# A third Winograd unit for the gates of a hybrid encoder layer, with the layer norm and the first rows reordered

## The chip, the core and the metric

The kernel runs on one core of a Trainium2 chip. The metric is the device time of one execution in microseconds (us). The engines that matter here are TensorE (PE; its weight loads, PEld, are listed apart and overlap the matmuls), VectorE (DVE), ScalarE (ACT), GpSimd (POOL) and SyncE (SP), which issues most of the DMAs.

## What is computed

One encoder layer on 512 tokens of width 1024: a gated pair of mixers (an S5 state-space branch and a gMLP branch), then cross-attention to 256 memory tokens, then a SwiGLU feed-forward network of width 2816. Only the first part is touched by the change:

```python
n = rms_norm(h, mix_norm_g[i])
proj = n @ w_in[i]                                  # 1024 x 4608
xa = proj[..., :OFF_U]                              # 512 columns, to S5
zu = proj[..., OFF_U:OFF_V]                         # 1024
zv = proj[..., OFF_V:OFF_GA]                        # 1024
gate_a = sigmoid(proj[..., OFF_GA:OFF_GB])          # 1024
gate_b = sigmoid(proj[..., OFF_GB:])                # 1024
ya = s5_branch(xa, ...)                             # ends y * sigmoid(gelu(y) @ w_glu)
yb = sgu_branch(zu, zv, ln_g, ln_b, w_s, bias)      # gelu(zu) * (w_s @ layer_norm(gelu(zv)) + bias)
merged = gate_a * (ya @ w_proj_a[i]) + gate_b * (yb @ w_proj_b[i])
h = h + merged @ w_out[i]
```

All matrices are float32.

## The kernel before

**Products.** Each float32 operand is split in two parts, hi and lo (`split`, L85 a ScalarE copy, L86 a VectorE subtraction), and each block product is three matmuls: hi by hi, hi by lo, lo by hi. `tokm` makes a result with tokens on the partitions (tiles `pt`, L393): the rows of 128 tokens are stationary, 512 columns of the weight stream by. `feat` makes a result with features on the partitions (tiles `pf`): one call gives 256 columns for all 512 tokens by 48 matmuls of 512 columns, and calls `evac` for each half. Where a product is large enough, the kernel uses Winograd's form of Strassen's scheme: a unit of 512 columns in seven block products instead of eight, each of 24 matmuls of 256 columns (`product`, L1221; tiles `gx`, `gv`, `gq` for the gates). The block products 1, 2, 4 and 7 read the features xn as they are; 3, 5 and 6 read sums of quarters of xn that `gate_sum` prepares. Their weights are blocks of w_in, or sums of these in the tile `gw`, made by VectorE or by an accumulating DMA.

**Stages, in TensorE's order.** First rows (rms norm, transposition `ptr` to features, L554); first half of zv, xa and second half of zv; the gate of a (`ga_evac`, four `feat` passes: sigmoid, tile `gas`, stored to the DRAM scratch `gad`); the spatial mixing (`psv`, L1185); zu, w_proj_b (result in `part`); the gate of b in two Winograd units, multiplied into `part` by `gate_put`; w_glu; w_proj_a, whose evacuation reads the gate of a back from `gad` (`gat`); then w_out, attention and the feed-forward network, which the change does not touch. The S5 branch runs as a side program: a generator whose steps are issued between the others', as `tick` counts the time of the matmuls issued. `later(n, f)` issues f after n of these time units. The S5 steps named below are `pw` (transposes, copied by ScalarE to `inx` or `ex`, L930), `pz` (copied to `zh`, L953), `pk` (copied to `ks`, L881), and the DMAs `kd` and `tt` (L889 to L897) on POOL's queue.

**Order.** Weights come in the order of `plan`: a block is loaded three blocks ahead (`LOADS`) or as many as its entry says, at most seven (`FAR`), and split two ahead (`SPLITS`). SP issues DMAs in the order in which they were issued in the program, POOL likewise. `plan_sums` spreads over the plan the sums that attention and the last projection need: a SP load or copy of a block into a DRAM tile `qsum`, then an accumulating load on POOL (L311). Its list of places says at which block of the plan each begins. `in_order` pins instructions to program order; all others a scheduler may move.

**The first rows.** `first_rows` broadcasts the norm's gain g by two matmuls (`pg`), copies each half to `g_mix` (L615) and then scales the half of row 0 (L616). In the loop over rows 1 to 3 each is scaled and turned. The log step of S5 comes by a DMA into a part of `slab` and is exponentiated at L726.

**The spatial mixing.** After the second half of zv, `row_weights` sums the rows of w_s. During the gate of a, `mixing_setup` (at `later(5)`) transposes w_s (`pws`), brings the layer norm's gain and bias to the partitions (`pgb`, `gbc`), scales `mix` (the broadcast row sums) by the bias of the norm (L1159) and adds `sgu_bias` by an accumulating DMA on POOL (L1160). `layer_norm(t)` at `later(1 + t)` subtracts the mean of row tile t (L1118), takes squares (`sq`, L515), a power on POOL (L1123), and scales (L1124). `psv` then takes the eight heads in turn; VectorE evacuates each with `mix` added (`sv`, L1186).

Of the kernel before, what the change touches and what calls it, by code (L numbers as in the profile page):

```python
# [52 lines left out]
def hybrid_layer_kernel(  # L53
# [29 lines left out]
    def split(dst_hi, dst_lo, src):  # L83
# [3 lines left out]
        if pinned[0]:  # L87
            in_order(hi)
            in_order(lo)


    pinned = [False]
# [130 lines left out]
    GATES = [(w_in, OFF_GB), (w_in, OFF_GB + 512)]  # L223
    ORDER = ((1, 0), (2, 0), (5, 0), (6, 0), (1, 1), (7, 0), (2, 1), (5, 1), (6, 1), (3, 0), (7, 1), (4, 0), (4, 1), (3, 1))
    gate_place = [None]

    def plan_gates():

        kh = KD // 2
        for q, i in ORDER:  # L230
            w, c0 = GATES[i]
# [12 lines left out]
            def make(q=q, i=i, b=b, got=got):  # L244
                t, b11 = (gate_place[0](2 * i + j) for j in range(2))
                if q in (2, 3):
                    return halves(got.pop("raw"))
                if q == 5 and i == 0:
                    nc.vector.tensor_tensor(t, t, got.pop("b12"), ALU.add)
# [3 lines left out]
                elif q == 6:  # L253
# [4 lines left out]
            loads = {1: [(5, whole(2 * i + 1, b(0, 0)))], 2: [(LOADS, plain(b(1, 0)))],  # L258
                     5: [(8, whole(2 * i, b(0, 0))),
                         (4, plain(b(0, 1), nm="b12")) if i == 0 else  # L260
                         (6, lambda i=i, b=b: nc.gpsimd.dma_start(gate_place[0](2 * i), b(0, 1), accum_op=ALU.add)),
# [72 lines left out]
    for c0 in range(0, D, 256):  # L334
        plan_feat(w_in, OFF_GA + c0, KD)
# [5 lines left out]
    for c0 in range(0, SW, 256):  # L341
        plan_feat(w_glu, c0, SW // P)
# [10 lines left out]
    for i in range(4):  # L353
# [7 lines left out]
    plan_sums([(5 + 3 * i, 3) for i in range(8)] + [(50 + 2 * i, 2) for i in range(7)] +  # L361
              [(85 + 3 * i, 3) for i in range(3)] + [(122 + 5 * i, 4) for i in range(14)])
# [69 lines left out]
    def tokm(w, c0, act, nk, evac, ntok=NT, last=2, kpt=2, hook=None, cut=None, t0=0):  # L432
# [19 lines left out]
        for t in toks:  # L452
# [5 lines left out]
            else:  # L458
                tok_block(ps[t], t, held, act, kpt, full, nw == last, True)
# [88 lines left out]
    def to_feat(src, hi, lo, tsl, full=None, skip=None, part=(0, 1), behind=None):  # L548

        for q in part:  # L550
            ps = aux("ptr", (P, 4, P))
            for j in range(4):
                k = 4 * q + j
                tr = nc.tensor.transpose(ps[:, j, :], src[:, k * P:(k + 1) * P], ident)  # L554
                if behind is not None:
                    in_order(tr)
            if q != skip:
                split(hi[:, 4 * q:4 * q + 4, tsl], lo[:, 4 * q:4 * q + 4, tsl], ps)
# [48 lines left out]
    def first_rows():  # L607
# [4 lines left out]
        idles(2)  # L612
        r = rms_factor(row_sums(xt[:, 0, :]))
        for i in range(2):
            in_order(nc.scalar.copy(g_mix[:, HALF[i]], pg[i]))  # L615
            in_order(nc.vector.scalar_tensor_tensor(xt[:, 0, HALF[i]], xt[:, 0, HALF[i]], r, pg[i], ALU.mult, ALU.mult))  # L616
# [1304 lines left out]
```

## Time and profile before

| | |
|---|---|
| runs | 875.28 us median of 3 (872.94 to 876.23) |
| profiled execution | 875.6 us; span of its instructions 873.8 us |
| mean granted TensorE clock | 0.991 |
| instructions | 14852 |
| TensorE busy | 860.3 us (98%), 5897 matmuls |
| VectorE, ScalarE, GpSimd busy | 648.0 (74%), 475.6 (54%), 108.8 (12%) |
| DMA | 155.40 MB, 178 GB/s on the mean |

The stages that the change touches, with the busy time of each engine in them (from the profile's windows):

```profile
0.00:22.60 22.60, 19.15 (x70) 14.30 (x71) 11.95 (x29) 13.09 (x29) 3.47 (x13) 0.85 0.81 237
22.60:97.80 75.20, 75.20 (x419) 61.37 (x418) 64.78 (x127) 38.41 (x68) 3.67 (x3) 0.98 0.61 161
97.80:154.00 56.20, 56.20 (x541) 46.50 (x540) 42.05 (x89) 37.64 (x64) 29.32 (x43) 1.00 0.68 184
161.20:265.40 104.20, 104.18 (x714) 85.23 (x712) 73.20 (x87) 54.35 (x64) 22.33 (x46) 1.00 0.53 138
265.40:305.80 40.40, 40.40 (x345) 40.40 (x345) 31.39 (x34) 26.18 (x37) 3.86 (x3) 1.00 0.72 194
```

A row gives the stretch in us from the span's start, its length, and the busy time and number of instructions of PE, PEld, DVE, ACT and POOL; then the granted TensorE clock (1.00 is full), the share of DMA time, and GB/s. The rows are the start; zv and xa; the gate of a; zu and w_proj_b; the gate of b. In the rows of timelines below, the start and the duration come first, then engine, line, operation and tiles, and in brackets the idle time of that engine ahead of it with what ended it. In rows of the chain it is start, duration and what the chain ran through. In grouped rows, busy time and mean duration in ns follow the count, then idle time ahead of the group.

### The profile page before, as it was taken

How to read it: one execution, taken by the hardware profiler on the slowest of the kernel's cores; microseconds unless marked ns; L12 is line 12 of the kernel's file. 1: busy time of each engine (PE TensorE's matmuls, PEld its weight loads, DVE VectorE, ACT ScalarE, POOL GpSimd, SP SyncE). 2: the span in 40 equal slices, each digit the busy share in tenths (PEclk: the TensorE clock that was granted, in tenths of full speed). 3: DMA queues.
4: the chain of work that ended last, by engine and by line, in shares of the span. 5: the costliest groups of instructions: out<-in, count | busy, mean ns of one | idle time of the engine just before them, and what ended most of it. 6: DMA issues, size and time to landing. Idle time of an engine off the chain costs nothing.

```text
span 873.8 us, 14852 instructions
## 1 busy us (share of the span) xinstructions
PE 860.3 (98%) x5897; PEld 764.8 (88%) x5897; DVE 648.0 (74%) x897; ACT 475.6 (54%) x704; POOL 108.8 (12%) x157
## 2 busy tenths in 40 slices
PE   8999999999999999999999999999999999999996
PEld 6788888878889988889899878999999999888875
DVE  5599679867748768679658656867877778889875
ACT  5453875267436544557547444645545454655663
POOL 1000066100611010110000001001111111000000
PEclk8999999999999999999999999999999999999998
DMA  7457559844647687934688144557799777467672
GB/s 235 121 154 223 115 179 234 203 121 153 173 121 197 162 223 202 287 113 167 204 253 218 54 151 110 145 135 177 173 222 228 201 194 167 135 205 229 197 249 85
DMA packets 110119, 155.40 MB, mean 178 GB/s; under 512 B 8969, under 2 KB 77089, under 8 KB 109986
## 3 DMA queue, kind: packets, MB, share of 16 engines
q1 hardware_dynamic: 91746, 128.27, 45.1%
q0 software_dynamic: 18016, 25.66, 18.5%
q8 instruction: 46, 0.75, 0.3%
q10 hardware_dynamic: 288, 0.52, 0.2%
q14 instruction: 23, 0.19, 0.1%
HBM read 148.70 MB, written 37.20 MB: 213 GB/s over the span
## 4 chain that ended last, share of the span: by engine, by line
PE 95%; DVE 1%; DMA 1%; SPq 1%; ACT 0%; issue 0%; POOLq 0%; POOL 0%; ACTq 0%
PE pf L393 27%; PE pt L393 18%; PE px L1221 12%; PE dx L393 7%; PE pq L1221 6%; PE dq L393 3%; PE pv L1221 3%; PE gx L1221 3%; PE qx L1221 2%; PE dv L393 2%; PE py L1015 1%; DMA slab<-in_s_log_step_dram 1%; PE gq L1221 1%; PE ptr L554 1%; PE po L393 1%; PE qq L1221 1%
## 5 line engine op out<-in xcount | busy, mean ns | idle before, releaser
L86 DVE TENSOR_TENSOR wlo<-wraw,whi 128x1024 fp32r<-128x1024 f32 (+1 forms) x135 | 160.0, 1185 | 82.4 <-ACT whi L85 82.0
L85 ACT CAST whi<-wraw 128x1024 fp32r<-128x1024 f32 (+1 forms) x135 | 138.0, 1023 | 145.0 <-PE pf L393 46.9
L393 PE MATMUL pf<-xn,whi 128*128 128x512 f32 x320 | 100.4, 393 | 0.0
L1221 PE MATMUL px<-fn,whi 128*128 128x256 f32 x480 | 83.3, 276 | 0.0
L1221 PEld LDWEIGHTS px<-fn,whi 128*128 128x128 f32 x480 | 72.5, 188 | 0.3 <-ACT u L1776 0.2
L393 PEld LDWEIGHTS pf<-xn,whi 128*128 128x128 f32 x320 | 59.5, 188 | 12.7 <-issue 0.7
L86 DVE TENSOR_TENSOR wlo<-b,whi 128x1024 fp32r<-128x1024 f32 x40 | 48.9, 1222 | 28.9 <-ACT whi L85 28.9
L85 ACT CAST whi<-b 128x1024 fp32r<-128x1024 f32 x40 | 42.2, 1054 | 51.2 <-PE px L1221 27.1
L1221 PE MATMUL px<-fn,wlo 128*128 128x256 f32 x240 | 66.4, 277 | 0.0
L393 PE MATMUL pf<-xn,wlo 128*128 128x512 f32 x160 | 62.6, 392 | 0.0
L393 PE MATMUL dx<-whi,s 128*128 128x512 f32 x170 | 53.9, 392 | 1.4 <-ACT whi L85 1.0
L1221 PE MATMUL pq<-s,whi 128*128 128x256 f32 x320 | 55.1, 276 | 0.0
L86 DVE TENSOR_TENSOR wlo<-t,whi 128x1024 fp32r<-128x1024 f32 x30 | 36.7, 1224 | 19.9 <-ACT whi L85 19.9
L85 ACT CAST whi<-t 128x1024 fp32r<-128x1024 f32 x30 | 31.6, 1053 | 35.8 <-PE pv L1221 12.6
L1221 PEld LDWEIGHTS pq<-s,whi 128*128 128x128 f32 x320 | 48.3, 188 | 0.1
L393 PE MATMUL pt<-whi,xn 128*128 128x512 f32 x128 | 45.4, 430 | 1.9 <-ACT xn L85 1.9
L1221 PEld LDWEIGHTS px<-fn,wlo 128*128 128x128 f32 x240 | 45.1, 188 | 0.0
L1221 PE MATMUL pq<-s,wlo 128*128 128x256 f32 x160 | 44.2, 277 | 0.0
L393 PEld LDWEIGHTS dx<-whi,s 128*128 128x128 f32 x170 | 31.7, 188 | 8.5 <-ACT whi L85 1.2
L393 PEld LDWEIGHTS pf<-xn,wlo 128*128 128x128 f32 x160 | 30.1, 188 | 6.3 <-issue 0.2
L311 POOL DMA_DIRECT2D dsum<-in_w_down_dram x12 | 13.3, 1108 | 163.3 <-DMA dsum<-in_w_down_dram 163.3
L393 PE MATMUL dx<-wlo,s 128*128 128x512 f32 x85 | 33.1, 390 | 0.0
(478 smaller groups left out, 2342.4 us busy)
## 6 DMA issues: line engine op xcount, KB each, us to landing
wraw<-in_w_in_dram SPq DMA_DIRECT2D x35, 512.0 KB, 5.4
dsum<-in_w_down_dram SPq DMA_DIRECT2D x20, 512.0 KB, 5.7
wraw<-dsum SPq DMA_DIRECT2D x20, 512.0 KB, 3.9
b<-in_w_gate_dram SPq DMA_DIRECT2D x15, 512.0 KB, 4.8
b<-in_w_up_dram SPq DMA_DIRECT2D x15, 512.0 KB, 4.5
wraw<-in_w_down_dram SPq DMA_DIRECT2D x15, 512.0 KB, 4.0
dsum<-in_w_down_dram POOLq DMA_DIRECT2D x10, 512.0 KB, 7.7
dsum<-dsum POOLq DMA_DIRECT2D x10, 512.0 KB, 5.5
```

What stands on the lines that cost most here:

```text
L85: hi = nc.scalar.copy(dst_hi, src)
L86: lo = nc.vector.tensor_tensor(dst_lo, src, dst_hi.bitcast(F32), ALU.subtract)
L311: plan[j + step][1].append((0, lambda d=dst, x=more: nc.gpsimd.dma_start(d, x, accum_op=ALU.add)))
L393: nc.tensor.matmul(ps, a[x], b[y], start=start and i == 0, stop=stop and i == 2, skip_group_check=free)
L554: tr = nc.tensor.transpose(ps[:, j, :], src[:, k * P:(k + 1) * P], ident)
L1015: in_order(nc.tensor.matmul(ps[64 * j:64 * j + 64, :], a, b, start=g % 4 == k == 0, stop=k == 2, tile_position=(0, 64 * j), skip_group_che ...
L1221: nc.tensor.matmul(ps[:, j, :], a[x], b[y], start=start and j == k == i == 0, stop=k == 3 and i == 2, skip_group_check=True)
```

## The change

It has four parts. (1) The second half of the columns of the gate of a leaves the `feat` passes and becomes a third Winograd unit beside the two of the gate of b: `GATES` has three entries, `ORDER` 21 products and the two passes of w_glu among them. The unit's tiles for weights and the bank of its fifth product are shared with those of the second unit of b, and its results go through SP to `gad`. (2) `layer_norm(t)` follows the evacuation of row tile t of zv's second half, `mixing_setup` is put off by 4.6 units from before that second half, and only two `feat` passes of the gate of a are left ahead of `psv`. (3) In `first_rows` row 0 is scaled ahead of the copies of g; the copies, the split of the first block and the features of row 0 are pinned in a new order; rows 1 to 3 are scaled behind the features of the row before; the split of the third weight block, the first matmuls of the last two weight blocks, the Exp of the log step and the row sums of w_s are held behind named instructions. (4) The places of `plan_sums` are moved.

```diff
-    GATES = [(w_in, OFF_GB), (w_in, OFF_GB + 512)]
-    ORDER = ((1, 0), (2, 0), (5, 0), (6, 0), (1, 1), (7, 0), (2, 1), (5, 1), (6, 1), (3, 0), (7, 1), (4, 0), (4, 1), (3, 1))
+    GATES = [(w_in, OFF_GA + 512), (w_in, OFF_GB), (w_in, OFF_GB + 512)]
+    ORDER = ((1, 0), (1, 1), (2, 0), (2, 1), (5, 0), (6, 0), (5, 1), (7, 0), (6, 1), (3, 0), (7, 1), (4, 0), (4, 1),
+             (1, 2), (3, 1), (5, 2), (6, 2), (2, 2), (7, 2), (0, 0), (4, 2), (3, 2), (0, 256))
...
-                t, b11 = (gate_place[0](2 * i + j) for j in range(2))
+                t, b11 = (gate_place[0](2 * (i % 2) + j) for j in range(2))
...
-    for c0 in range(0, D, 256):
+    for c0 in range(0, 512, 256):
         plan_feat(w_in, OFF_GA + c0, KD)
...
-    plan_sums([(5 + 3 * i, 3) for i in range(8)] + [(50 + 2 * i, 2) for i in range(7)] +
-              [(85 + 3 * i, 3) for i in range(3)] + [(122 + 5 * i, 4) for i in range(14)])
+    plan_sums([(5 + 5 * i // 2, 3) for i in range(8)] + [(53 + 2 * i, 2) for i in range(7)] +
+              [(88 + 3 * i, 3) for i in range(3)] + [(125 + 5 * i, 4) for i in range(14)])
...
-        idles(2)
         r = rms_factor(row_sums(xt[:, 0, :]))
-        for i in range(2):
-            in_order(nc.scalar.copy(g_mix[:, HALF[i]], pg[i]))
-            in_order(nc.vector.scalar_tensor_tensor(xt[:, 0, HALF[i]], xt[:, 0, HALF[i]], r, pg[i], ALU.mult, ALU.mult))
...
+        for i in range(2):
+            in_order(nc.vector.scalar_tensor_tensor(xt[:, 0, HALF[i]], xt[:, 0, HALF[i]], r, pg[i], ALU.mult, ALU.mult))
         for q in range(2):
-            split(hi[:, q, :], lo[:, q, :], raw[:, q, :])
+            in_order(nc.scalar.copy(hi[:, q, :], raw[:, q, :]))
+            in_order(nc.scalar.copy(g_mix[:, HALF[q]], pg[q]))
             to_feat(xt[:, 0, :], xn_hi, xn_lo, slice(0, P), part=(q,))
+            in_order(nc.vector.tensor_tensor(lo[:, q, :], raw[:, q, :], hi[:, q, :].bitcast(F32), ALU.subtract))
...
-        rms_scale(xt[:, t, :], g_mix, xt[:, t, :], ss)
+        r = rms_factor(ss)
+        with tc.issue_after(turned[1].ins):
+            for i in range(2):
+                scaled = nc.vector.scalar_tensor_tensor(xt[:, t, HALF[i]], xt[:, t, HALF[i]], r, g_mix[:, HALF[i]], ALU.mult, ALU.mult)
...
+            with tc.issue_after(scaled.ins):
+                split_w(2)
+            turned1 = row_tr[0]
...
+        stp = small()
+        with tc.issue_after(last_row[0]):
+            A_.activation(stp, ls, AF.Exp)
...
-    tokm(w_in, OFF_V, xn, KD, zv_evac(0))
+    tokm(w_in, OFF_V, xn, KD, zv_evac(0), behind=turned1)
...
-        nc.vector.tensor_reduce(rs, wsr, AX.X, ALU.add)
+        with tc.issue_after(last_row[1]):
+            nc.vector.tensor_reduce(rs, wsr, AX.X, ALU.add)
...
+    def zv_last(t, ps):
+        zv_evac(1)(t, ps)
+        later(0.4, lambda: layer_norm(t))
+
     gbcs = []
     row_weights()
-    later(5, lambda: gbcs.append(mixing_setup()))
-    for i in range(NT):
-        later(1 + i, lambda i=i: layer_norm(i))
-    for c0 in range(OFF_GA, OFF_GB, 256):
+    later(4.6, lambda: gbcs.append(mixing_setup()))
+    tokm(w_in, OFF_V + 512, xn, KD, zv_last)
+    for c0 in range(OFF_GA, OFF_GA + 512, 256):
         feat(w_in, c0, xn, KD, ga_evac)
...
     def gate_put(i, f, ts, src):
 
-        m = 4 * i + 2 * f
+        if i == 0:
+            m = 4 + 2 * f
+            nc.sync.dma_start(gad[m:m + 2, :, ts].rearrange("m p t -> p m t"), src)
+            return
+        m = 4 * (i - 1) + 2 * f
         V.tensor_tensor(part[:, m:m + 2, ts], part[:, m:m + 2, ts], src, ALU.mult)
...
-        if n == 8:
+        if n == 10:
             finish_side()
...
+        if q == 0:
+            if not ya:
+                ya = [s5p.tile([P, 4, T], F32R, tag=tag, name=name) for tag, name in (("u", "ya_hi"), ("zh", "ya_lo"))]
+            feat(w_glu, i, yg, 4, glu_evac)
+        else:
+            gate_step(q, i)
```

The places at which the sums `gsum` are made move by two passes of w_proj_b.

More of the change, by code (lines that the diff above doesn't have):

```diff
@@ L722, in s5_setup @@
         st["c"] = (cr, ci)
[L725 to L726 removed]
+        a, rho, th, n, sn, hs, cs = (small() for _ in range(7))
         V.tensor_tensor(a, lr, stp, ALU.mult)
```

64 lines of the change are left out of this document (33 added, 31 removed).

## Prediction

> **What bounds the kernel now.** I read the page first: the busy shares, the row of granted clocks, and the chain that ended last.
>
> ```profile
> PE 860.3 (98%) x5897; PEld 764.8 (88%) x5897; DVE 648.0 (74%) x897; ACT 475.6 (54%) x704; POOL 108.8 (12%) x157
> PEclk8999999999999999999999999999999999999998
> PE 95%; DVE 1%; DMA 1%; SPq 1%; ACT 0%; issue 0%; POOLq 0%; POOL 0%; ACTq 0%
> ```
>
> TensorE is busy for 860.3 of 873.8 us and carries 95% of the chain. So an edit gains only by fewer or cheaper matmuls or by taking away one of the few idle stretches, and it loses by opening a new one. The profiled execution took 875.6 us, 1.8 over its span; the median of the runs is 875.28, 0.3 lower. I make the sum from 875.6 and take 0.3 off.
>
> Next the chain of waits in order of time. First the stretches where TensorE is late or where the change counts matmuls:
>
> ```profile
> 5.97 11.27 DMA slab<-in_s_log_step_dram
> ...
> 17.47 0.58 ACT xn L85
> ...
> 18.09 7.15 PE pt L393 x23
> ...
> 131.12 0.35 PE pk L864 x8
> 131.47 0.10 PE pk L871 x15
> 131.57 0.45 PE pk L864 x16
> ...
> 137.29 0.16 PE pgb L1154
> 137.46 16.55 PE pf L393 x72
> 154.00 7.14 PE psv L1185 x64
> 161.15 21.77 PE pf L393 x96
> ...
> 272.01 2.86 PE gv L1221 x24
> ...
> 303.04 2.74 PE gq L1221 x24
> ```
>
> Two things: at 18 us TensorE had waited for a DMA of the S5 parameters through ScalarE, and from 131.12 to 182.92 there is no hole: each piece starts where the last one ends.
>
> **Part 1, the start: gain 3.5 us.** The waits at the first rows, and the clock by windows:
>
> ```profile
> 6.75 0.59 ACT L615 COPY g_mix<-pg 128x512 f32<-128x512 f32 x1 [1.44 <-PE pg L611]
> 7.44 1.53 DVE L616 SCALAR_TENSOR_TENSOR xt<-xt,r,pg 128x512 f32<-128x512 f32 x2 [1.75 <-ACT g_mix L615]
> ...
> 18.09 0.50 PE L393 MATMUL pt<-whi,xn 128*128 128x512 f32 x1 [1.91 <-ACT xn L85]
> ```
>
> ```profile
> 15.70:19.11 3.41, 1.50 (x8) 1.10 (x8) 1.95 (x5) 1.78 (x6) 0.14 (x1) 1.00 0.36 53
> 19.14:22.56 3.42, 3.42 (x10) 2.68 (x9) 1.83 (x5) 0.61 (x3) 0.92 (x2) 0.50 1.00 293
> 36.21:39.62 3.41, 3.41 (x10) 2.63 (x10) 0.41 (x2) 2.09 (x4) 0.00 (x0) 0.50 0.55 123
> ```
>
> (In the windows the first figure is the length, the second TensorE's busy time, and the third from the end the granted clock.) The Exp of the log step (L726) stands on ScalarE ahead of the copies of row 1. It waits for the DMA issued at 5.97, which lands at 17.24, and so row 1's xn copy, long ready, starts at 17.47 and TensorE waits 1.91. The change holds the Exp behind row 3's copies, so these 1.91 us go. The window 15.70 to 19.11, in which TensorE worked 1.50 of 3.41, is followed by one at clock 0.50; half of 3.42 is 1.7 lost. With the stall gone I expect that half window to go too. The third half window (36.21) follows the group of plam and pbc transposes, which the new order spreads between matmuls; it can go (another 1.7) or stay, and I leave it. Scaling row 0 ahead of the copy of g brings its first features about 0.7 earlier (a g copy of 0.59 ahead of L616's first half), but the second half of the weight block comes no earlier, since it now stands in a fixed order behind xn's: I count 0.4 of it. Against that the order of TensorE is now fixed row by row: the transposes of rows 2 and 3 stand just ahead of the matmuls that read them, so each row waits for one copy of about 0.5 less what still runs, 0.25 each. 1.9 + 1.7 + 0.4 - 0.5 = 3.5. The ends are 2.0 (half window stays) and 5.5 (the third goes too). Of what moves with it: the fourth weight block's DMA goes behind dcol and wsx on SP, some 2 us later, and is read only after 72 matmuls, 16 us on; that covers it.
>
> [...]
>
> **Part 2, the gates: gain 2.1 us.** Two of the four feature passes of a's gates, 96 matmuls of 512 columns, take 21.77 (the row at 161.15, same shape). In their place stand seven products of 24 matmuls of 256 columns. Such a product on xn takes 2.86 (272.01) and one on a prepared sum 2.74 (303.04); with four and three of these, 4 x 2.86 + 3 x 2.74 = 19.66. Gain 2.1. The added preparing of sums (three VectorE adds of 1.15 to 1.2 and the same splits), the three more stores and reloads of gates through SP, and one more accumulate on POOL lie in a stage where VectorE has about a fifth of its time free, and the third unit reuses tiles freed some 11 us before. I count nothing there, 1.5 at worst if VectorE falls behind once. The glu passes, moved between the gates' last products, cost what they did.
>
> **Part 3, the shorter cover ahead of psv: loss 11.1 us.** This is the step that decides. In before the layer norms, the mixing setup and an S5 block ran beside four passes of a's gates, the last of them ending at 154.00. Now two remain: 154.00 - 21.77 = 132.2, less the pk work that now falls between the psv groups (the rows from 131.12 on and their tail, 1.1 to 1.4), so TensorE is ready for psv at 130.8 on before's clock (all times of this part are on it; the matmul order up to the end of zv is the same). What must be done by then is not less. ScalarE's part:
>
> ```profile
> L85 ACT CAST whi<-wraw 128x1024 fp32r<-128x1024 f32 x10 | 10.5, 1049 | 9.6 <-PE pf L393 9.6
> L953 ACT COPY zh<-pz 128x512 f32<-128x512 f32 x6 | 6.0, 1100 | 3.2 <-PE pz L948 3.2
> L515 ACT ACTIVATE sq<-zt 128x512 f32<-128x512 f32 x8 | 5.0, 626 | 2.0 <-DMA gad<-gas 1.9
> L1124 ACT ACTIVATE zt<-zt,r 128x1024 f32<-128x1024 f32 x4 | 4.5, 1147 | 0.6 <-POOL r L1123 0.6
> L1168 ACT ACTIVATE gas<-pf 128x512 f32<-128x512 f32 x7 | 4.0, 591 | 2.3 <-PE pf L393 1.9 <-ACT wsx L1152 0.3
> L930 ACT COPY ex<-pw 128x512 f32<-128x512 f32 x4 | 2.4, 603 | 0.0
> L1168 ACT ACT_TABLE_LOAD x1 | 1.3, 1283 | 0.0
> ```
>
> Per-row layer norm puts all of this straight behind zv: 8 sq (5.0), 4 zh (4.0), one last zt-nm (1.05), 4 zt by r (4.3), 2 whi (2.0), 4 ex (2.0), the table (1.3), 2 gas (1.1), the first ks and bd (1.5), each taken from start to start. That is 22.2 us without a gap from 100.5 to 122.7, where before left idle time. TensorE meets it at once: its last group of pw transposes needs a bank that the third of the ex copies frees, which comes at 118.6, and it is there at 115.6: **3.0 us**, between 1 and 4 by what ScalarE gets done before 100.5. So psv starts at 133.8.
>
> The second wait is the bias under psv's result. sv (VectorE) reads mix, and mix is finished by an accumulating DMA on POOL, behind a chain of others:
>
> ```profile
> 140.56 0.51 POOL L889 DMA_DIRECT2D kd<-ks  x1 [0.61 <-DMA qsum<-in_w_q_dram]
> ...
> 145.42 0.96 POOL L1160 DMA_DIRECT2D mix<-in_sgu_bias_dram  x1
> ...
> 153.15 0.53 POOL L897 DMA_DIRECT2D tt<-kd  x1 [1.18 <-DMA mix<-in_sgu_bias_dram]
> ```
>
> Beside it SP's and VectorE's rows, the DMA's landing, and the landing times of the qsum tiles:
>
> ```profile
> 126.01 0.53 SPq L310 DMA_DIRECT2D qsum<-qsum  x1
> 140.96 1.65 DVE L1159 TENSOR_SCALAR mix<-mix,gbc 128x128 f32<-128x128 f32 x8
> 154.93 0.75 DVE L1186 SCALAR_TENSOR_TENSOR sv<-psv,gbc,mix 128x512 f32<-128x512 f32 x1 [0.55 <-PE psv L1185]
> ```
>
> ```profile
> mix<-in_sgu_bias_dram POOLq DMA_DIRECT2D x1, 512.0 KB, 7.4
> DMA to landing us min/median/max: 3.6/7.0/11.3
> ```
>
> In before mix was issued at 145.42 and landed near 152.8, one us ahead of psv. In the changed order POOL comes to mix only behind the first S5 block's kd and tt, and the last tt waits for the accumulate into the last qsum (as at 153.15 a tt waited for mix, with which it has no data in common), which waits for a copy that SP issues behind the store of the second gas: 122.7, so 123.1. Then 7.0 for the copy, 7.0 for the accumulate, 0.6 for the tt: mix is issued at 137.7, lands at 145.1, and the first sv ends at 145.85. TensorE does five of the eight heads (7.14 x 5 / 8 = 4.5) and 1.1 of pk from 133.8 and stands at 139.4, its sixth head needing the bank of the first sv: **6.45 us**. If qsum takes 3.6 each, the scaling of mix decides: before ended it 5.3 after pgb, so 134.6 here, landing 142.5, and the wait is 3.8; with 11.3 for each it is 15. I take the medians, which the rows at 126.01 and 140.56 (14.55 from the copy to the accumulate's landing) bear out.
>
> [...] 3.0 + 6.45 + 1.7 = 11.1.
>
> **The sum.** 875.6 - 3.5 - 2.1 + 11.1 = 881.1, less 0.3: 880.8 us, slower by 0.6%. A measurement of this kernel can tell about 0.5%, 4.4 us, from no change.
>
> **The rivals.**
> - *The cover suffices.* mix lands before the sixth head and ScalarE keeps up, because the early layer norms draw ahead of 100.5 some of the work that I have in the backlog, and SP passes the qsum copy earlier. For it: mix's DMA is an accumulate of 7.4 that has only one scaling of 1.65 directly ahead of it, all else being its place in POOL's queue. Against it: mix would have to land by 138.6, so be issued by 131.2, before its own scaling is done by my reckoning (134.6). It decides where mix is issued before 131. Then 875.6 - 3.5 - 2.1 - 0.3 = 869.7. Chance 0.27.
> - *One wait only, small.* The pw wait is covered, or the qsum pair lands at 3.6 each, and no half clock follows: loss of 3.8 to 6.5 in place of 11.1, so 873.5 to 876.2, no change. For it: the least landing is 3.6; against it: the medians. Chance 0.2.
> - *Slower by more.* The qsum pair lands late (11.3 each), the wait is 15 in place of 6.45 with two half windows: 891. For it: this stretch moves more bytes at once, since the sums now start earlier. Chance 0.08.
> - *The new order of the start does nothing*: row 1's copy was waiting on something else as well. Then only 0.4 of the 3.5 comes, 883.9, within the forecast's case. The rows at 5.97 and 17.47 speak against it: the copy starts 0.2 after the landing.
>
> **How the numbers follow.** The forecast has 0.45 (876.3 to 887: the waits from 5 to 14 with the half window, the start from 2.0 to 5.5), the cover 0.27, the small wait 0.2, the long one 0.08. Faster by over 0.5% is below 870.9: nearly all of the first rival and a sliver of the second, 0.27. Within 0.5%, 870.9 to 879.7: the second rival and the lower part of the forecast's case, 0.27. Slower: 0.46. The range goes from 869 (which takes in the first rival's middle) to 888.
>
> **What would show it.** In the changed profile: the Exp of log step behind 20 us and the window at 19 us at clock 1.00; no wait of 1.9 at row 1; three runs of 24-matmul products per gate unit, 19.7 a unit; a row of pw or pz with a wait on ScalarE's ex near 115; and psv's sixth group, or the matmuls behind it, waiting some 4 to 8 us on VectorE's sv, whose own wait ends with the DMA of mix. If sv's wait ends with psv, and not with mix, part 3 is wrong, and the time is near 870.

## Result: slower by 1.7%, and the profile after

| | before | after |
|---|---|---|
| time, median of 6 runs | 874.21 us (872.86 to 876.23) | 889.5 us (884.9 to 892.84) |
| ratio | | 1.0166 (95% interval 1.0145 to 1.0187) |
| profiled execution, its span | 875.6, 873.8 us | 892.84, 891.1 us |
| mean granted clock | 0.991 | 0.986 |

The forecast was 880.8 in a range of 869 to 888, slower with a chance of 0.46. The direction was right, but the time lies above that range, and the slowing was more than double what was forecast. The executions of the changed kernel spread more widely than those of the kernel before, and the profiled one, from which all sizes below are read, is the slowest of the six: two others took 885 us with clocks of 0.991 and 0.993.

The page of the changed kernel: TensorE's work has grown only a little, its share has fallen, and a slice with a lower clock appears inside the span.

```profile
PE 864.7 (97%) x5965; PEld 769.9 (86%) x5965; DVE 655.2 (74%) x905; ACT 481.3 (54%) x712; POOL 103.8 (12%) x158
PEclk9999999999989999999999999999999999999998
```

TensorE's waits in the changed kernel (engine, line, what it waited for, us in all, times, longest). In the kernel before, none of the first five rows exists:

```profile
PE psv L1201 <- DVE sv L1202: 3.7, 2, 3.3
PE pw L944 <- ACT ex L945: 2.7, 1, 2.7
PE gx L1237 <- ACT u L1246: 2.4, 1, 2.4
PE gx L1237 <- DVE gse L86: 2.1, 1, 2.1
PE gx L1237 <- ACT gse L85: 1.1, 1, 1.1
```

The first two are the ones that the prediction named. The other three are at the gates, where the sum had counted nothing.

The granted clock around each wait, in pairs: the window with the wait and the one behind it (TensorE's busy time second, the clock third from the end):

```profile
111.15:114.56 3.41, 0.75 (x24) 0.47 (x13) 0.78 (x1) 3.38 (x6) 0.55 (x2) 1.00 0.68 177
114.56:117.97 3.41, 3.33 (x10) 2.85 (x11) 1.52 (x3) 3.31 (x9) 1.64 (x4) 0.50 0.29 104
138.46:141.87 3.41, 0.87 (x7) 0.87 (x8) 2.45 (x4) 0.00 (x0) 2.20 (x5) 1.00 0.81 228
141.87:145.28 3.41, 2.99 (x15) 2.70 (x14) 3.41 (x6) 0.00 (x0) 1.83 (x4) 0.50 0.11 28
257.92:261.33 3.41, 1.40 (x10) 1.00 (x9) 3.41 (x4) 2.97 (x4) 0.08 (x1) 1.00 0.49 166
261.33:268.16 6.83, 5.72 (x29) 5.50 (x31) 6.73 (x6) 0.58 (x1) 1.29 (x1) 0.50 0.75 156
315.95:319.36 3.41, 0.98 (x6) 0.56 (x5) 2.35 (x3) 3.37 (x5) 1.16 (x1) 1.00 0.10 38
319.36:322.77 3.41, 3.41 (x18) 3.41 (x17) 2.68 (x4) 1.74 (x3) 0.00 (x0) 0.50 0.91 120
```

At each of the four places (waits of 2.4 to 3.7 us in all, at 258 in two parts of 1.1 and 2.1) TensorE was busy for 1.4 us or less of a window of 3.41, and each was followed by a half clock, the one at 261 for two windows: five windows at 0.50, by my estimate 1.7 us lost in each (half of 3.41).

**Where the time went.** A second profile of the kernel before (below) is the better base, as its start is not disturbed. I cut the execution where TensorE starts the first pf, where it starts the last matmul of psv, and where it starts w_proj_a. First the kernel before in its second profile, then the changed kernel; the columns are those of the windows:

```profile
42.85:158.54 115.69, 115.10 (x910) 96.47 (x909) 99.98 (x189) 65.65 (x110) 33.68 (x47) 1.00 0.72 192
158.54:314.09 155.55, 155.55 (x1108) 134.74 (x1106) 112.89 (x129) 86.03 (x107) 27.59 (x50) 1.00 0.60 155
```

```profile
41.67:145.71 104.04, 97.62 (x819) 81.43 (x817) 83.07 (x136) 59.60 (x105) 23.76 (x39) 0.97 0.70 179
145.71:331.60 185.89, 180.23 (x1275) 158.94 (x1274) 137.55 (x190) 99.19 (x122) 32.14 (x58) 0.97 0.58 158
```

I call the two stretches "to psv" and "to w_proj_a". Two passes fewer should make the first 115.7 - 21.8 = 93.9 long; it took 104.0, so 10.1 are lost. Seven more products should make the second 155.55 + 19.66 = 175.2; it took 185.9, so 10.7 are lost. The earlier start gives 1.2, and the last projection took 2.7 more in this execution (small waits on VectorE and ScalarE, not explained). Part 4 moves sums that this projection reads, but in other runs with the same places of the sums it took as little as in before (114.0 us with the start undone, 114.3 at the pace of 0.92 with the old sums; 116.7 here, 114.0 in before's second profile), so I count it as scatter. -1.2 - 21.8 + 10.1 + 19.7 + 10.7 + 2.7 = 20.2, the difference of the last matmul's start (882.3 against 862.1).

### The profile page after: what moved, and what is told of

The parts are those of the page before. It is cut to its first block, busy times and chain, and to the rows that moved or that the text cites. A ratio compares the mean times of both kernels' runs of the same rounds, so it can differ in the third digit from the quotient of the medians.

```text
span 891.1 us, 15013 instructions
## 1 busy us (share of the span) xinstructions
PE 864.7 (97%) x5965; PEld 769.9 (86%) x5965; DVE 655.2 (74%) x905; ACT 481.3 (54%) x712; POOL 103.8 (12%) x158
## 4 chain that ended last, share of the span: by engine, by line
PE 84%; DMA 5%; DVE 4%; ACT 4%; issue 2%; POOL 0%; SPq 0%; POOLq 0%; ACTq 0%; DVEq 0%
PE pf L397 21%; PE pt L397 17%; PE px L1237 12%; PE pq L1237 6%; PE dx L397 4%; PE gx L1237 4%; PE pv L1237 3%; PE qx L1237 2%; PE gq L1237 2%; DVE wlo L86 2%; PE dq L397 2%; DMA wraw<-dsum 2%; PE py L1030 1%; PE po L397 1%; PE qq L1237 1%
## 5 line engine op out<-in xcount | busy, mean ns | idle before, releaser
L85 ACT CAST whi<-wraw 128x1024 fp32r<-128x1024 f32 x131 | 134.7, 1029 | 142.1 <-PE pf L397 43.6
L86 DVE TENSOR_TENSOR wlo<-wraw,whi 128x1024 fp32r<-128x1024 f32 x131 | 156.0, 1193 | 68.5 <-ACT whi L85 67.9
L397 PE MATMUL pf<-xn,whi 128*128 128x512 f32 x256 | 80.8, 395 | 0.0
L397 PEld LDWEIGHTS pf<-xn,whi 128*128 128x128 f32 x256 | 48.5, 190 | 10.2 <-issue 0.2
L397 PE MATMUL pf<-xn,wlo 128*128 128x512 f32 x128 | 51.1, 399 | 0.0
L397 PE MATMUL pt<-whi,xn 128*128 128x512 f32 x128 | 42.8, 407 | 0.3 <-ACT xn L85 0.2
L1237 PEld LDWEIGHTS pq<-s,wlo 128*128 128x128 f32 x160 | 30.1, 188 | 0.0
```

Of the source, the lines that this page charges most:

```text
L85: hi = nc.scalar.copy(dst_hi, src)
L86: lo = nc.vector.tensor_tensor(dst_lo, src, dst_hi.bitcast(F32), ALU.subtract)
L397: nc.tensor.matmul(ps, a[x], b[y], start=start and i == 0, stop=stop and i == 2, skip_group_check=free)
L1237: nc.tensor.matmul(ps[:, j, :], a[x], b[y], start=start and j == k == i == 0, stop=k == 3 and i == 2, skip_group_check=True)
```

## Experiments

The base of each ratio is the kernel before, run beside it. The last two columns are the two stretches in its profile.

| kernel | median us | ratio (95% interval) | to psv | to w_proj_a |
|---|---|---|---|---|
| before, second profile | 872.73, one run | | 115.7 | 155.6 |
| after | 889.5 | 1.0166 (1.0145 to 1.0187) | 104.0 | 185.9 |
| start alone | 875.6 | 1.0009 (0.9998 to 1.0019) | 115.5 | 159.3 |
| start and layer norm | 878.23 | 1.0033 (1.0017 to 1.0050) | 120.2 | 155.4 |
| start undone | 891.26 | 1.0193 (1.0161 to 1.0224) | 103.4 | 183.0 |
| idle matmuls, before | 881.81 | 1.0075 (1.0053 to 1.0098) | 121.1 | 156.9 |
| idle matmuls, after | 887.55 | 1.0155 (1.0127 to 1.0183) | 103.9 | 182.9 |
| bias by VectorE | 894.0 | 1.0218 (1.0199 to 1.0237) | 101.5 | 189.1 |
| last weight sum by VectorE | 887.41 | 1.0143 (1.0121 to 1.0166) | 103.8 | 181.5 |
| sums earlier | 886.46 | 1.0147 (1.0120 to 1.0174) | 104.4 | 179.4 |
| both of these | 886.5 | 1.0120 (1.0097 to 1.0143) | 104.3 | 177.8 |
| scalings held | 891.6 | 1.0187 (1.0166 to 1.0209) | 103.5 | 187.0 |
| pace 0.92 | 887.47 | 1.0136 (1.0114 to 1.0157) | 103.5 | 181.5 |
| pace, old sums, weight sum | 881.87 | 1.0070 (1.0053 to 1.0087) | 103.6 | 176.6 |
| all of these | 881.11 | 1.0064 (1.0048 to 1.0081) | 99.8 | 177.9 |
| all, mixing set up earlier | 882.66 | 1.0106 (1.0085 to 1.0127) | 94.8 | 184.7 |
| the same without the third unit | 876.75 | 1.0032 (1.0019 to 1.0044) | 117.3 | 157.8 |

### What each part of the change does

**The start alone.** The kernel before with the edits of the first rows, the Exp and the row sums.

> The kernel before with the change's part for the first rows alone (scaling ahead of the copies of g, the pinned order, the Exp and the row sums held back). Theory: the changed kernel reaches the gate of a 3.7 us earlier than before (94.06 against 97.76), and nothing behind gives it back: 874.2 - 3.7 = 870.5, ratio 0.996. Rival: the 3.7 are lost again in the S5 side program, which starts later: 873 to 875.

It gains nothing that can be measured. Its first pf comes at 41.74, but at the gates TensorE waits 1.9 us for a split (`PE gx <- DVE wlo`), a window at clock 0.50 follows (275.01 to 278.42, behind one with 1.56 us of work in 3.41), and "to w_proj_a" is 3.7 longer than in before's second profile. The number is the rival's; that a later start of S5 is the reason is not shown. To tell whether the first profile of before was typical, I took a second one.

> The kernel before, unchanged, for a second profile of it. Theory: the 1.9 us wait at row 1 and the two half-clock windows at 19.1 and 36.2 of the first profile belong to that execution (the DMA of the log step landed at 17.24), and the kernel with the idle matmuls, which starts alike, had neither; here the gate of a begins at 42 to 43 and not at 46, and the gates wait somewhere for 1 to 4 us instead. Rival: they belong to the kernel, and the first pf comes at 46 again.

```profile
15.70:19.11 3.41, 2.68 (x14) 2.06 (x13) 2.76 (x7) 2.42 (x7) 0.55 (x1) 1.00 0.59 124
19.14:22.56 3.42, 3.42 (x19) 2.82 (x18) 1.30 (x4) 0.00 (x0) 0.55 (x1) 1.00 1.09 321
```

The same windows as those of the prediction: here the Exp waited 0.56 for its DMA and not 1.82, TensorE was busy for 2.68 of 3.41 in the first window and not 1.50, and no half clock follows, nor one at 36. The first pf starts at 42.85 (46.04 in the first profile). So 3.2 of the 4.4 us between before's first profile and the changed kernel were of that one execution. The gates waited nowhere in this profile, so that half of my expectation was wrong. All the profiles together say that the start scatters: in the four with the old start (these two, the idle matmuls before, the start undone) the first pf comes between 42.0 and 46.0, in the sixteen with the new one between 41.2 and 43.5. The half clock at 36 is not of that execution alone: it is there again with the start undone, where the Exp waited 1.17 and there is no half clock at 19, so it does not hang on that wait.

**The layer norm too.** The start alone, with the layer norm per row tile; four passes and two units as before.

> The kernel before with the changed start and the layer norm per row tile, but the gate of a in four passes and two units for the gates of b, as before: the changed kernel without its third unit, and with the old places of the sums. Theory (it is the third unit, by taking 21.8 us of cover from ahead of psv, that loses; the layer norm per row costs nothing under four passes): 873 to 877, ratio 1.000. Rival (the early layer norm fills ScalarE and opens the pw wait by itself): that wait of 2.8 and a half window show here too, 879 to 881.

The rival's mechanism was right: the pw wait (2.7) is there under four passes too, with its half clock (0.50 from 116.23 to 119.64, behind a window with 0.90 us of work), and the time is some 3 us over before (879 to 881 was its number). The wait belongs to the layer norm, and the third unit is not needed for it. What the third unit, its shorter cover and the new places of the sums of part 4 add is the rest, from 1.0033 to 1.0166. Part 4 was not tried alone.

**The start undone** in the changed kernel: its edits to the first rows, the Exp and the row sums put back.

> The changed kernel with the first rows, the Exp and the row sums as in the kernel before. Theory (what is saved ahead of psv is lost again at the waits of psv and of the gates): 888 to 890.5, no worse than the changed kernel. Rival (gains add up): 889.5 + 3.7 = 893.

Its median is 1.8 above that of the changed kernel, with intervals that overlap: this does not tell the two theories apart.

### Is TensorE the bound?

24 matmuls that nobody reads, ahead of psv:

```diff
+    extra = bank("extra")
+    for i in range(24):
+        nc.tensor.matmul(extra, xn_hi[:, 0, 0:P], xn_hi[:, i % KD, :], start=True, stop=True)
```

> The kernel before with 24 idle matmuls of 512 columns (24 x 0.227 = 5.45 us of TensorE work, its result read by nobody) just ahead of psv. Theory (TensorE alone bounds the kernel before in this stretch): the time grows by all of it, 874.9 + 5.4 = 880.3, ratio 1.006. Rival (VectorE's chain through S5 and the sums of the gates is about as late as TensorE already, as the start alone gave nothing back): the 5.4 are swallowed in part, 876 to 878.

> The changed kernel with the same 5.45 us of idle TensorE work at the same place. Theory (TensorE waits there for others, and again at the gates): psv's wait of 3.3 and the clock's half window go, and the gates' waits shrink, so the time grows by nothing or falls: 884 to 890, ratio 1.011 to 1.018. Rival (the waits are of a fixed length behind TensorE's own work): 889.5 + 5.4 = 895.

Before pays for all of them (7.0 in the medians: the 5.45, and 1.6 more, as a wait of 1.6 at the gates appears). The changed kernel pays nothing: 887.55. TensorE's own work bounds the one ahead of psv and not the other.

### Taking single waits away

**The bias by VectorE**: in place of the accumulating DMA,

```diff
-            nc.vector.tensor_scalar(mix[:, h_, :], mix[:, h_, :], gbc[...], None, ALU.mult)
-        nc.gpsimd.dma_start(mix..., sgu_bias..., accum_op=ALU.add)
+            nc.vector.scalar_tensor_tensor(mix[:, h_, :], mix[:, h_, :], gbc[...], bia[:, h_, :], ALU.mult, ALU.add)
```

> The changed kernel, but the bias of the spatial mixing comes by a plain load into a free part of wsx, early, and VectorE adds it while it scales mix (one instruction per head as before); the accumulating DMA on POOL is gone. Theory: psv's 3.3 us wait ends with that DMA (issued 135.0, landed 140.1), so mix is ready at about 134.8, the wait goes, and with it the half-clock window at 141.9 (1.7): 889.5 - 3.7 - 1.7 = 884, ratio to before about 1.011. Rival: VectorE's queue is what is late at 131 to 143, and sv comes no earlier: 888 to 890, and psv still waits for sv.

psv's last matmul starts 2.9 us earlier and the half clock behind it is gone (the granted clock over "to psv" is 0.98, 0.97 in the changed kernel). A wait of 2.6 for sv stays, behind VectorE's S5 operations. At the gates everything is lost again, and more: there TensorE now waits 6.5 for ScalarE's copy of gse (1.1 in the changed kernel) and 2.7 for u.

**The last weight sum by VectorE**, from the block that is loaded anyway:

```diff
+                    if q == 2 and i == 2:
+                        nc.vector.tensor_tensor(t, t, raw, ALU.add)
...
+                    if i != 2:
+                        nc.gpsimd.dma_start(t, b(1, 0), accum_op=ALU.add)
```

> The changed kernel, but the third unit's last weight sum (for its fourth product) is made by one VectorE add of the block that its second product has loaded anyway, in place of an accumulating DMA on POOL. Theory: that DMA took 10.7 us (305.25 to 315.9) and ScalarE, in order behind the split that waits for it, kept back the copies that the next product needs: the 2.4 us wait at 316.5 and the half-clock window at 319.4 (1.7) go: 889.5 - 4.1 = 885.4, ratio about 1.013. Rival: one more 1.2 us add on a loaded VectorE puts the same wait behind VectorE: 888 to 890.

As expected in the profile (181.5, so 4.4 less); in the medians half of that, with intervals that overlap. The mechanism in the changed kernel, in rows of POOL's and ScalarE's timelines:

```profile
305.25 1.77 POOL L260 DMA_DIRECT2D gw<-in_w_in_dram  x1
...
315.93 1.05 ACT L85 CAST whi<-gw 128x1024 fp32r<-128x1024 f32 x1 [8.95 <-DMA gw<-in_w_in_dram]
...
318.30 0.59 ACT L1246 COPY u<-gx 128x512 f32<-128x512 f32 x1
```

ScalarE stands for 8.95 us before the split that needs the DMA; the copy of u stands behind it in ScalarE's order, and TensorE waits for u.

**The sums of features earlier**, each one pass of w_proj_b sooner; then **both** of these.

```diff
-        if n > 1:
-            gate_sum(n - 2)
-    gate_sum(2)
+        if n > 0:
+            gate_sum(n - 1)
```

> The changed kernel, but the three sums of features for the gates are made one pass of w_proj_b earlier. Theory: VectorE works without a gap from 239.6 to 264 and the split that product 6 needs (gse) comes 3.4 us late, which also halves the clock from 261.3 to 268.2 (3.4): 889.5 - 6.8 = 882.7, ratio about 1.010. Rival: the S5 side program still holds the tiles or VectorE until 232, so the sums come no earlier, or S5 is late in their place: 888 to 892.

> The changed kernel with two mendings at once: the sums of features one pass of w_proj_b earlier, and the third unit's last weight sum on VectorE. Theory: each took 4 us or more out of the gates (pf of w_proj_a began 6.3 and 4.3 earlier), and the wait behind ScalarE's u of the first still holds 1.6, which the second takes away: 889.5 - 6.4 - 2 to 4 = 879 to 881, ratio 1.005 to 1.007. Rival: both waits are of the same lateness of VectorE, and it shows once only: 884 to 886.

The two half windows at 261 go (the granted clock over "to w_proj_a" is 1.00 in both kernels, 0.97 in the changed kernel) and "to w_proj_a" falls by 6.5, with the last weight sum by 8.1 in all. The profiled executions took 884.95 and 884.48 us and the medians are 886.46 and 886.5, so the medians show only 3 of it, and for both together no more than for the sums alone: 879 to 881 was expected, and the rival's 884 to 886 is nearer. In the changed kernel, VectorE's rows show what was late:

```profile
255.57 1.22 DVE L1285 TENSOR_TENSOR x<-x,xn 128x1024 f32<-128x1024 f32 x1
257.15 0.69 DVE L1318 TENSOR_TENSOR part<-part,gs 128x512 f32<-128x512 f32 x1 [0.36 <-ACT gs L1323]
257.76 1.22 DVE L259 TENSOR_TENSOR gw<-gw 128x1024 f32<-128x1024 f32 x1
258.89 2.35 DVE L86 TENSOR_TENSOR wlo<-gw,whi 128x1024 fp32r<-128x1024 f32 x2
261.16 1.22 DVE L86 TENSOR_TENSOR gse<-x,gse 128x1024 fp32r<-128x1024 f32 x1
```

The last sum (L1285) ends at 256.8, and its split (gse) comes at 261.16 behind other operations, with no gap to speak of. VectorE's first sum and the split, in before's second profile and then the first sum in the changed kernel:

```profile
227.91 1.22 DVE L1246 TENSOR_TENSOR x<-xn 128x1024 f32<-128x1024 f32 x1
...
260.81 1.23 DVE L86 TENSOR_TENSOR gse<-x,gse 128x1024 fp32r<-128x1024 f32 x1
```

```profile
240.71 1.22 DVE L1262 TENSOR_TENSOR x<-xn 128x1024 f32<-128x1024 f32 x1
```

The split comes at the same time in both (260.81 and 261.16), but TensorE begins the gates at 257.4 in before and at 243.9 in the changed kernel. The first sum starts 29.5 us ahead of the gates in before and 3.2 ahead of them in the changed kernel, where the edit asks for the sums two passes of w_proj_b later. One pass earlier, as here, it starts at 232.5, and the split at 253.64.

**The scalings held** behind the last copies of ex, so that these come first on ScalarE:

```diff
+        def scale():
+            with tc.issue_after(pwc[-1].ins):
+                nc.scalar.activation(z, z, AF.Copy, scale=r)
+        later(2.4, scale)
```

The first try kept the factor r of the four rows in a new tile of 4 bytes a partition, with four buffers.

> The changed kernel, but the four scalings of the layer norm (zt by r) are held behind the last copy of ex in ScalarE's queue. Theory: the pw wait of 2.8 is ScalarE's backlog, in which these 4.3 us stand ahead of the copies; it goes, and the half window at 114.6 (1.7) with it: psv begins 4 us earlier; the sv wait then takes part of it back, since mix lands when it did: 887 to 889.5, and at the gates no better. Rival: the copies wait for something else (the transposes, DVE), and the pw wait stays: 889 to 891.

It took 901.85 us (1.0301, 1.0268 to 1.0334), and all mendings so far together with that tile took 900.41 (1.0286, 1.0253 to 1.0318).

> The changed kernel with all four mendings: bias by VectorE, last weight sum by VectorE, sums of features one pass earlier, scalings held behind the ex copies. Theory: the waits taken away one by one were pw 2.8, psv 3.3, gse 3.4 and u 2.4 and five half windows of 1.7, some 20 us in the profile; half of what is won ahead of the gates comes back there as VectorE is late: 876 to 881, ratio 1.002 to 1.007. Rival A: nothing comes back, and the third unit gives its 2.1: 872. Rival B: VectorE's work ahead of the gates is the bound, all comes back: 885 to 888.

The profiles say why neither tells of the waits: the loss is behind the touched stages. A group of the feed-forward network in the first try, and the same group with r in a free column of zsum (count, busy us, mean ns):

```profile
L1245 PE MATMUL px<-fn,whi 128*128 128x256 f32 x426 | 76.4, 281 | 0.0
```

```profile
L1245 PE MATMUL px<-fn,whi 128*128 128x256 f32 x436 | 75.3, 276 | 0.0
```

> The changed kernel with the scalings of the layer norm held behind the ex copies, as in the run before, but with the factor kept in a column of zsum that is free by then, so that no new tile moves the others: in that run each feed-forward matmul took 279 to 281 ns in place of 276. Theory: the pw wait goes, the sv wait grows by as much (6.8 there), and the gates are as late as they were: 888 to 891, the matmuls at 276. Rival: the hold itself slows the rest, 895 to 902.

Now the pw wait is gone and psv begins at 127.34 (131.93 in the changed kernel), but TensorE waits 7.1 for sv and psv ends where it did. The qsum copy and POOL's issue behind it, which the prediction put ahead of mix, are in the chain of this kernel, and so is mix's DMA, with VectorE's scaling of mix from its timeline below them:

```profile
120.57 7.30 DMA qsum<-qsum
128.49 1.29 POOL qsum L317
129.78 1.49 issue
...
131.28 8.07 DMA mix<-in_sgu_bias_dram
```

```profile
129.33 1.65 DVE L1180 TENSOR_SCALAR mix<-mix,gbc 128x128 f32<-128x128 f32 x8
```

POOL was through with the qsum at 129.78. The scaling ends at 130.98, and mix is issued 0.3 behind it, as in the changed kernel (134.73 and 135.02). So the scaling decides when mix starts, here too, and not the qsum; the longer wait is psv's earlier start and a DMA of 8.07 in place of 5.04.

### Pace or load?

`RATE` sets how much of the S5 side program is issued for each us of matmuls. I raised it from 0.8 to 0.92, alone and with the sums of features at the places that they had before the change and the last weight sum by VectorE.

```diff
-    RATE = 0.8
+    RATE = 0.92
...
-        if n > 1:
-            gate_sum(n - 2)
-    gate_sum(2)
+        gate_sum(n)
```

> The changed kernel with the pace of the S5 side program raised from 0.8 to 0.92 of TensorE's time. Theory: the side program is paced by the matmuls issued, and the change has taken 21.8 us of these away ahead of psv, so its last steps and the sums that use its tiles fall to the gates (VectorE half idle at 200 to 240, then without a gap to 264); a quicker pace brings them back into 200 to 240: the gse wait of 3.4 and its two half windows go, 883 to 885. Rival: VectorE is simply full, or the quicker pace makes the psv stage worse by as much: 888 to 891.

> The changed kernel with that pace, the sums of features at their old places (a pass of w_proj_b earlier again than in the mended kernel above), and the last weight sum on VectorE. Theory: no wait is left at the gates: from psv to w_proj_a the time is that of the matmuls, which leaves the pw and sv waits and their half windows: 889.5 - 11 = 878 to 881, ratio 1.004 to 1.007. Rival: 885, as the mended kernel at pace 0.8.

VectorE (third busy time) in the changed kernel, with the pace alone, and in the second of these:

```profile
200.00:235.00 35.00, 34.88 (x339) 28.23 (x337) 17.88 (x18) 23.93 (x27) 4.61 (x12) 1.00 0.41 126
235.00:262.00 27.00, 24.32 (x168) 22.07 (x162) 24.44 (x23) 15.03 (x19) 14.91 (x29) 0.99 0.59 153
```

```profile
200.00:235.00 35.00, 35.00 (x325) 28.90 (x322) 25.95 (x27) 21.32 (x27) 10.27 (x23) 1.00 0.60 164
235.00:262.00 27.00, 27.00 (x234) 25.21 (x234) 23.39 (x21) 16.78 (x19) 9.88 (x18) 1.00 0.45 120
```

```profile
200.00:235.00 35.00, 34.08 (x335) 27.91 (x334) 28.71 (x29) 22.51 (x28) 6.83 (x16) 1.00 0.49 140
235.00:262.00 27.00, 26.93 (x178) 24.48 (x178) 19.98 (x19) 15.99 (x20) 11.98 (x24) 1.00 0.54 151
```

VectorE did 17.9 us of work in the 35 that end 9 ahead of the gates and was then nearly full. With the quicker pace alone it did 25.95 there, the first sum starts at 228.7 and the split of gse at 251.43, and TensorE does not wait for gse. The time was forecast too low even so (887.47 against 883 to 885): a wait of 3.6 for u stays, and the wait for sv grows from 3.7 to 7.1. With the earlier sums and the last weight sum too, VectorE did 28.7, and TensorE has no wait at the gates ("to w_proj_a" 176.6 against 175.2 of pure work). VectorE's work in "to w_proj_a" is nearly the same, 137.55 us in the changed kernel and 135.66 here, so it was the place of that work and not its amount. The time is 881.9, just above what was expected.

### Are gains ahead of psv kept then?

Three kernels: the last one with the bias by VectorE and the scalings held as above; this with the mixing set up earlier; and this again without the third unit, with four passes and two units as before.

```diff
-    later(4.6, lambda: gbcs.append(mixing_setup()))
+    later(3.4, lambda: gbcs.append(mixing_setup()))
```

> The same with the bias by VectorE and the scalings held too, the factor in zsum: all mendings at once. Theory: with the gates clear, what is won ahead of psv is kept: 878 to 881 less 4 to 8 = 871 to 876, ratio 0.997 to 1.001. Rival (what is won ahead of the gates comes back there, as with the bias alone): 880 to 886.

> The kernel with all mendings, and the mixing setup 1.2 units (6 us) earlier, so that mix is ready before VectorE takes up the S5 scan. Theory: psv's last wait (3.5, sv behind the scan in VectorE's queue) and its half window (1.7) go, and with the gates clear they are kept: 881.1 - 5.2 = 876, ratio 1.001. Rival: VectorE only exchanges one lateness for another, and the gates wait again: 880 to 882.

> The same mendings without the third unit: the kernel before with the changed start, the layer norm per row tile with its scalings held, the bias by VectorE, the early mixing setup and the pace of 0.92, under four passes of the gate of a and two units. Theory (with every wait gone the third unit would be worth its 2.1 us, and this kernel is 2 slower than the fully mended one): 874 to 878 where that one is at 876. Rival (TensorE waits nowhere here, as it has 21.8 us of cover more): 871 to 873, faster than all others, and the third unit never pays.

The first two expectations (871 to 876, and 876) were missed; the rivals, by which the gain comes back at the gates, are nearer. The third (874 to 878) was met, though the kernel with the third unit, which it put at 876, is at 882.66. With the bias and the scalings added, "to psv" is 3.8 shorter and "to w_proj_a" 1.3 longer; the median falls by 0.8, inside the intervals. With the mixing set up 6 us earlier, `later(3.4)`, psv has no wait left, and "to psv" is the 94 of pure work:

```profile
42.04:136.82 94.78, 94.78 (x819) 79.32 (x817) 77.74 (x129) 59.54 (x105) 18.86 (x30) 1.00 0.76 196
136.82:321.54 184.72, 178.18 (x1275) 156.74 (x1274) 145.15 (x198) 100.39 (x124) 34.92 (x65) 0.99 0.59 157
```

But VectorE brings 145.15 us of work into the second stretch (135.66 with the quicker pace, the old sums and the weight sum), TensorE waits there for ScalarE (2.5) and VectorE (2.3), and all 5.0 that were won come back as 6.8. Over both stretches the kernel with pace, old sums and weight sum, the one with all mendings and the one with the earlier mixing take 280.2, 277.7 and 279.5 us, where TensorE's work is 269.1. Without the third unit the same mendings leave no wait of TensorE over 0.8 between the start and the last projection and take 876.75, 5.9 less than with it. So in no tried form did the third unit pay, and no tried version beats the kernel before. Which link of S5 keeps VectorE from doing more between 100 and 130 (14.7 of 30 us with the third unit and the earlier mixing) was not tried.

## Why the prediction was right in direction and too small

The step that failed is in part 2: the price of nothing for VectorE's added work at the gates, where 10.7 us were lost. Part 1 failed too, and part 3 came out near its number partly by luck.

**Part 3, the psv stage: right, 11.1 forecast, 10.1 measured.** The pw wait is 2.75 in its row of the timeline against 3.0, for the reason given: ScalarE was in arrears, and holding its scalings took the wait away. Two terms had the wrong size and by luck nearly cancel. The sv wait was 3.7 and not 6.45: of the two ends I took the one by the medians of the qsum DMAs, and it was the other (3.8), where the scaling of mix on VectorE decides:

```profile
133.66 1.07 DVE mix L1172 x5
134.73 0.29 issue
135.02 5.04 DMA mix<-in_sgu_bias_dram
...
140.19 0.75 DVE sv L1202
```

The 1.7 for the clock, one half window behind the longer of the two waits, stood on no run: the longest wait of TensorE in before's profile is 1.9. The changed kernel's profile showed two half windows in this stage, one behind each wait, 2.75 and 3.25 us long. In the runs with the scalings held or the quicker pace, too, mix was issued 0.3 behind its scaling, so the chain by qsum that I priced was never seen to decide.

**Part 1, the start: wrong, 3.5 forecast, nothing measured.** The failed step is that a wait for a DMA's landing, and the half window behind it, were priced as the kernel's from one execution. The Exp's DMA landed some 1.2 us earlier in the second. What is left (1.2 between that profile and the changed kernel, 2.1 between the means of the four old starts and the sixteen new ones) does not show in the time when the part stands alone, 875.6 against 874.9; in its profile 3.7 are lost at the gates. The ends that I gave this part, 2.0 and 5.5, should by its own terms have been 1.8 and 5.2.

**The clock.** The windows shown with 0.75 to 1.50 us of work in 3.41, so 1.9 to 2.7 without, were all followed by clock 0.50, as was the one with 1.56 in the start alone; the window with 2.68 was followed by 1.00. In the changed kernel the clock's changes from 114.56 to 322.77 lie 3.41 us or a whole multiple of it apart. Cut at these distances from 40 us on, all other windows of its profile at full clock, but one at the end of the kernel (1.45, followed by 0.50), had 2.40 us of work or more, and 1.00 followed. The length of the wait alone does not tell the two cases apart: 1.91 us in before's first profile had a half window behind it, and with the start undone TensorE waited 3.2 for u across the edge of two windows, and the clock stayed at 1.00:

```profile
315.03:318.44 3.41, 1.73 (x8) 1.11 (x6) 0.40 (x1) 1.47 (x3) 0.00 (x0) 1.00 0.84 258
318.44:321.86 3.42, 1.88 (x15) 1.88 (x16) 3.16 (x4) 2.31 (x5) 1.16 (x1) 1.00 0.33 19
321.86:325.27 3.41, 3.41 (x32) 3.41 (x31) 2.93 (x4) 2.40 (x5) 0.00 (x0) 1.00 1.05 230
```

Not explained are two half windows of before's first profile: the one at 36.21 follows a window with 3.41 of work in 3.41, and the one at 8.90 a window with 3.29. In these runs, then, a wait of some 3 us came with 1.7 for the clock (pw, 2.75) or with nothing (u, 3.2), and the range of such a wait should have held both.

**Part 2, the gates: the step that failed.** The matmuls' price held (175.2 against 176.6 where nothing waits). "I count nothing there, 1.5 at worst" was wrong by 10.7 in the profile: 3.2 and two half windows at gse, 2.4 and one at u. I took VectorE's share of idle time in that stage as cover. That is a share over a stage, and the change itself moved work into the front of it. It asks for the sums of features two passes of w_proj_b later, a move that I gave no term. And the side program is paced by matmuls issued, 21.8 us of which were gone ahead of psv, so its steps, the sums that use its tiles, and the splits met between 235 and 262, while TensorE came to the gates 13.4 us earlier. Sums one pass earlier, or a quicker pace alone, each took the wait for gse away. The wait for u had another cause, the accumulating DMA ahead of ScalarE's split, and went with it. I also costed the cover that the two passes gave up for psv alone; it was cover for everything that S5 and VectorE had to do before the gates.

**The rivals.** "The cover suffices" asked for mix to be issued before 131; it was at 135.0. "One wait only, small" has the right sv wait, but there were five waits. The start that "does nothing" has the right number for the first part, and was given no chance of its own; its reason, that row 1's copy waited for something else as well, is not what the runs show. The sum with the measured terms, from the first profile's 875.6: start 4.4, third unit 2.1, psv 10.1, gates 10.7, last projection some 2.5, gives 892.4; that execution took 892.84, and the median is 3.3 lower.

## What to carry to other kernels

When work is taken from an engine that is busy for 98%, ask what that work was hiding, and not only at the next wait: here a second chain that was hidden with little to spare came out at the gates, and in most tries what was won ahead of them came back there. Where steps are paced by another engine's work, taking that work away delays them against it; sum the second engine's work between the two places where it must be done, and price each move in the order as well. Take a second profile before a wait for a DMA is priced.

## What the runs showed of the hardware

With a new tile of 4 bytes a partition, with four buffers, the seven costliest groups of 128x256 matmuls of the feed-forward network, which does not use it, took 279 or 281 ns a matmul, in both kernels that had the tile; in the changed kernel they took 276. From 600 to 760 us of the span TensorE made 1368 matmuls with the tile and 1423 in the changed kernel. With the same value in an existing tile they took 276 again. What it is about the tile that does this was not tried by itself.

In the changed kernel the granted clock was 0.50 behind the windows of 3.41 us in which TensorE was busy for 0.75, 0.87, 0.98 and 1.40 us. With the start undone, a wait of 3.2 us lay in two windows with 1.73 and 1.88 us of work, and the clock behind each was 1.00.
